# RMSNorm with swish on one core: row groups of unequal size, and three engines kept in the written order

## The chip, the cores and the metric

The kernel runs on one core of a Trainium2 chip. The time is device microseconds of one execution. Four engines matter here: ACT (ScalarE), DVE (VectorE), POOL (GpSimd), and SP (SyncE), which only issues DMA transfers in this kernel. TensorE does nothing.

## What is computed

`x` is 16 x 1024 x 512 float32, so 16384 rows of 512 values, `gamma` has 512 values and `eps` is a number.

```
rms = np.sqrt(np.mean(x ** 2, axis=-1, keepdims=True) + eps)
x_norm = x / rms * gamma
return (x_norm * (1.0 / (1.0 + np.exp(-x_norm)))).astype(np.float32)
```

## The kernel before

Each of the 128 partitions holds 128 whole rows, one after the other in memory. They are worked on in 16 tiles of `R = 8` rows a partition, so a tile is 128 x 4096 float32, 2.097 MB. A tile stays in one buffer `x_t` of a pool of eight from its load to its store; all steps work in place on it.

A tile goes through these steps, each written as a function with the tile's number:

- `issue_load` (L66): SP issues one transfer from HBM into `x_t`.
- `stage_sq` (L76): ACT squares each of the 8 rows and sums it into a column of `ms`, one instruction a row.
- `stage_rstd` (L89, L93): POOL adds eps to `ms` and raises it to the power -0.5, giving `rstd`, two small instructions of 128 x 8.
- `stage_z_sig` (L107, L116): DVE multiplies each row by its `rstd` and by `gamma`, one instruction a row; then ACT takes the sigmoid of the whole tile into `s_t` (two buffers).
- `stage_mul` (L128): DVE multiplies `x_t` by `s_t`, one instruction for the tile.
- `stage_store` (L139): SP issues one transfer back to HBM.

The loop at the end runs steps s = 0, 1, ...; in each it writes load s + 2, sq s, rstd s - 1, z and sigmoid s - 2, product s - 3, store s - 4. That is the order in which the work is written. The order in which each engine gets it is set by the framework's scheduler, which sorts ready work by its own estimate of times; on each engine the work is then done strictly in the order that came out, and waits are on semaphores. SP's queue is in order too: a transfer that waits holds back those behind it. In the order that came out, SP issues `gamma` and seven loads without a wait, and from there on a store and a load in turns; a load also waits until the store that last used its buffer has landed.

Each DMA transfer is spread over 16 DMA engines, and the transfers of one queue go through each of these one behind the other.

Of the kernel before, what the change touches and what calls it, by code (L numbers as in the profile page):

```python
# [1 line left out]

# [4 lines left out]

FP32 = mybir.dt.float32


@with_exitstack
def kernel(
    ctx: ExitStack,
    tc: tile.TileContext,
    x: bass.AP,
    gamma: bass.AP,
    eps: bass.AP,
    out: bass.AP,
):
    nc = tc.nc  # L20
    P = nc.NUM_PARTITIONS

    eps_val = float(eps)

    xf = x.flatten_outer_dims()
    of = out.flatten_outer_dims()
    N, D = xf.shape
    assert N % P == 0
    RPP = N // P
    x_v = xf.rearrange("(p n) d -> p n d", p=P)  # L30
    o_v = of.rearrange("(p n) d -> p n d", p=P)

    R = 8
    while RPP % R != 0:
        R //= 2
    R = max(R, 1)
    ntiles = RPP // R

    consts = ctx.enter_context(tc.tile_pool(name="consts", bufs=1))
    xpool = ctx.enter_context(tc.tile_pool(name="xpool", bufs=8))  # L40
    spool = ctx.enter_context(tc.tile_pool(name="spool", bufs=2))
    small = ctx.enter_context(tc.tile_pool(name="small", bufs=6))
    scratch = ctx.enter_context(tc.tile_pool(name="scratch", bufs=4))

    g_t = consts.tile([P, D], FP32)
    nc.sync.dma_start(out=g_t[:], in_=gamma.partition_broadcast(P))

    neghalf = consts.tile([P, R], FP32)
    nc.gpsimd.memset(neghalf[:], -0.5)  # L49
    eps_t = consts.tile([P, R], FP32)  # L50
    nc.gpsimd.memset(eps_t[:], eps_val)  # L51

    inv_sqrt_d = float(D) ** -0.5

    x_tiles: dict[int, bass.AP] = {}
    ms_tiles: dict[int, bass.AP] = {}
    rstd_tiles: dict[int, bass.AP] = {}
    s_tiles: dict[int, bass.AP] = {}

    PRE = 2  # L60

    def issue_load(i):
        if not (0 <= i < ntiles):
            return
        x_t = xpool.tile([P, R, D], FP32)
        nc.sync.dma_start(out=x_t, in_=x_v[:, i * R : (i + 1) * R, :])  # L66
        x_tiles[i] = x_t

    def stage_sq(i):
        if not (0 <= i < ntiles):  # L70
            return
        x_t = x_tiles[i]
        ms = small.tile([P, R], FP32)
        for r in range(R):
            sq_a = scratch.tile([P, D], FP32, tag="sqa")
            nc.scalar.activation(  # L76
                out=sq_a[:],
                in_=x_t[:, r, :],
                func=mybir.ActivationFunctionType.Square,
                scale=inv_sqrt_d,  # L80
                accum_out=ms[:, r : r + 1],
            )
        ms_tiles[i] = ms

    def stage_rstd(i):
        if not (0 <= i < ntiles):
            return
        ms = ms_tiles.pop(i)
        nc.gpsimd.tensor_tensor(  # L89
            out=ms[:], in0=ms[:], in1=eps_t[:], op=mybir.AluOpType.add  # L90
        )
        rstd = small.tile([P, R], FP32)
        nc.gpsimd.tensor_tensor(  # L93
            out=rstd[:],
            in0=ms[:],
            in1=neghalf[:],
            op=mybir.AluOpType.pow,
        )
        rstd_tiles[i] = rstd

    def stage_z_sig(i):
        if not (0 <= i < ntiles):
            return
        x_t = x_tiles[i]
        rstd = rstd_tiles.pop(i)
        for r in range(R):
            nc.vector.scalar_tensor_tensor(  # L107
                out=x_t[:, r, :],
                in0=x_t[:, r, :],
                scalar=rstd[:, r : r + 1],  # L110
                in1=g_t[:],
                op0=mybir.AluOpType.mult,
                op1=mybir.AluOpType.mult,
            )
        s_t = spool.tile([P, R, D], FP32)
        nc.scalar.activation(  # L116
            out=s_t[:],
            in_=x_t[:],
            func=mybir.ActivationFunctionType.Sigmoid,
        )  # L120
        s_tiles[i] = s_t

    def stage_mul(i):
        if not (0 <= i < ntiles):
            return
        x_t = x_tiles[i]
        s_t = s_tiles.pop(i)
        nc.vector.tensor_tensor(  # L128
            out=x_t[:],
            in0=x_t[:],  # L130
            in1=s_t[:],
            op=mybir.AluOpType.mult,
        )

    def stage_store(i):
        if not (0 <= i < ntiles):
            return
        x_t = x_tiles.pop(i)
        nc.sync.dma_start(out=o_v[:, i * R : (i + 1) * R, :], in_=x_t[:])  # L139

    for i in range(PRE):
        issue_load(i)

    nsteps = ntiles + 4
    for s in range(nsteps):
        issue_load(s + PRE)
        stage_sq(s)
        stage_rstd(s - 1)
        stage_z_sig(s - 2)
        stage_mul(s - 3)  # L150
        stage_store(s - 4)


# [1 line left out]
_INS = ['x', 'gamma', 'eps']  # L155
_OUTS = [((16, 1024, 512), 'float32')]
#: Inputs that are plain numbers.
_NUMBERS = {'eps': 9.999999747378752e-06}


# [26 lines left out]
```

## Time and profile before

| | |
|---|---|
| time, median of 4 runs | 201.62 us (201.45 to 201.84) |
| time of the profiled execution | 201.55 us |
| its span in the trace | 199.6 us |
| DVE busy | 155.1 us, 144 instructions |
| ACT busy | 138.5 us, 274 instructions |
| POOL busy | 58.9 us, 38 instructions |
| moved by DMA | 67.40 MB |

The span runs from the first to the last event of the core in the trace; the time of the execution is some 2 us longer. A time or a wait below is in microseconds from the span's start. The rows on which the prediction rests stand in a section of their own below.

### The profile page before, as it was taken

To read this page: it belongs to the slowest core of one execution; us is meant where nothing else is said; L and a number is where in the kernel's file an instruction comes from. 1 tells how busy PE (TensorE), PEld (TensorE's weight loads), DVE (VectorE), ACT (ScalarE), POOL (GpSimd) and SP (SyncE) were. 2 spreads that over 40 slices of the span, in tenths; PEclk is the share of its full clock that TensorE was granted. 3 is DMA by queue.
4 is the path that set the end of the run, shared out by engine and by line. 5 is a ranking of instruction groups with operands and counts; after the bars stand their busy time and mean duration, and the time that the engine had idled before them with its cause. 6 is when DMAs were issued, how large, how long until landed. Compare 5 with 4: busy or idle time off the path is not lost.

```text
span 199.6 us, 599 instructions
## 1 busy us (share of the span) xinstructions
DVE 155.1 (78%) x144; ACT 138.5 (69%) x274; POOL 58.9 (29%) x38
## 2 busy tenths in 40 slices
DVE  0004996999999999999969997899699967559350
ACT  2089799999999999529793976079956922940600
POOL 0003506408255283910584029100440030030000
DMA  5999999999999999999999999977910494054036
GB/s 151 424 430 424 437 437 425 417 433 404 368 305 433 435 420 427 424 427 437 414 432 427 430 427 433 433 322 332 446 72 0 210 420 210 0 210 210 0 151 269
DMA packets 4755, 67.40 MB, mean 338 GB/s; under 512 B 528, under 2 KB 528, under 8 KB 656
## 3 DMA queue, kind: packets, MB, share of 16 engines
q1 hardware_dynamic: 4752, 67.37, 81.0%
q14 instruction: 3, 0.02, 0.0%
HBM read 33.82 MB, written 33.55 MB: 337 GB/s over the span
## 4 chain that ended last, share of the span: by engine, by line
issue 40%; POOL 22%; DVE 5%; ACT 3%; POOLq 1%
POOL ms L89 12%; POOL rstd L93 9%; DVE x_t L107 3%; DVE x_t L128 2%; ACT s_t L116 2%; ACT sq_a L76 1%; POOLq L182 1%; POOLq L93 0%
## 5 line engine op out<-in xcount | busy, mean ns | idle before, releaser
L107 DVE SCALAR_TENSOR_TENSOR x_t<-x_t,rstd,g_t 128x512 f32<-128x512 f32 x128 | 86.2, 746 | 29.9 <-POOL rstd L93 29.9
L116 ACT ACTIVATE s_t<-x_t 128x4096 f32<-128x4096 f32 x16 | 57.8, 3611 | 40.1 <-DVE x_t L107 40.1
L76 ACT ACTIVATE sq_a<-x_t 128x512 f32<-128x512 f32 x128 | 78.4, 614 | 8.7 <-DMA x_t<-in_x_dram 8.7
L128 DVE TENSOR_TENSOR x_t<-x_t,s_t 128x4096 f32<-128x4096 f32 x16 | 70.5, 4419 | 7.4 <-ACT s_t L116 7.4
L89 POOL TENSOR_TENSOR ms<-ms,eps_t 128x8 f32<-128x8 f32 x16 | 28.9, 1806 | 118.2 <-ACT sq_a L76 118.2
L93 POOL TENSOR_TENSOR rstd<-ms,neghalf 128x8 f32<-128x8 f32 x16 | 29.6, 1853 | 1.3
L76 ACT ACTIVATION_READ_ACCUMULATOR sq_a<-x_t 128x1 f32 x128 | 23.9, 187 | 0.0
L76 ACT ACT_TABLE_LOAD x1 | 1.3, 1283 | 0.7 <-PEq L168 0.7
L116 ACT ACT_TABLE_LOAD x1 | 1.3, 1283 | 0.0
L49 POOL MEMSET neghalf<- 128x8 f32 x1 | 0.1, 106 | 0.3 <-POOLq L168 0.3
L168 POOL MEMSET const-float32-0.0<- 128x1 f32 x1 | 0.1, 99 | 0.2 <-issue 0.2
L51 POOL MEMSET eps_t<- 128x8 f32 x1 | 0.1, 105 | 0.0
L168 POOL MEMSET const-bfloat16-1.0<- 128x1 bf16 x1 | 0.1, 102 | 0.0
L168 POOL MEMSET const-uint8-127<- 128x1 uint8 x1 | 0.1, 102 | 0.0
L168 POOL MEMSET const-float32-1.0<- 128x1 f32 x1 | 0.1, 99 | 0.0
## 6 DMA issues: line engine op xcount, KB each, us to landing
x_t<-in_x_dram SPq DMA_DIRECT2D x16, 2048.0 KB, 15.3
out_dram<-x_t SPq DMA_DIRECT2D x16, 2048.0 KB, 11.5
g_t<-in_gamma_dram SPq DMA_DIRECT2D x1, 256.0 KB, 4.9
```

The lines of the kernel that those rows point to most:

```text
L49: nc.gpsimd.memset(neghalf[:], -0.5)
L51: nc.gpsimd.memset(eps_t[:], eps_val)
L76: nc.scalar.activation(out=sq_a[:], in_=x_t[:, r, :], func=mybir.ActivationFunctionType.Square, scale=inv_sqrt_d, accum_out=ms[:, r : r + 1],)
L89: nc.gpsimd.tensor_tensor(out=ms[:], in0=ms[:], in1=eps_t[:], op=mybir.AluOpType.add)
L93: nc.gpsimd.tensor_tensor(out=rstd[:], in0=ms[:], in1=neghalf[:], op=mybir.AluOpType.pow,)
L107: nc.vector.scalar_tensor_tensor(out=x_t[:, r, :], in0=x_t[:, r, :], scalar=rstd[:, r : r + 1], in1=g_t[:], op0=mybir.AluOpType.mult, op1= ...
L116: nc.scalar.activation(out=s_t[:], in_=x_t[:], func=mybir.ActivationFunctionType.Sigmoid,)
L128: nc.vector.tensor_tensor(out=x_t[:], in0=x_t[:], in1=s_t[:], op=mybir.AluOpType.mult,)
L168: nc = _bacc.Bacc("TRN2", target_bir_lowering=False, num_devices=1)
L182: with _tile.TileContext(nc) as tc:
```

## The change

Three things change.

The tiles get unequal sizes. `R` becomes the list `sizes`: 2, 2, 4, 4, 4 rows, then twelve tiles of 8, then 4, 4, 4, 2, 2, together 128 rows in 22 tiles. Each buffer keeps its full size (`RMAX` = 8 rows) and a small tile uses the first part of it. The pool of `x_t` grows from 8 to 9 buffers, that of `ms` and `rstd` from 6 to 8.

What stands ahead of the loop moves. The first two loads are written first; `gamma` is then loaded from ACT's queue, not SP's; the two constants of POOL's step are filled by DVE, not POOL; and a sigmoid of 128 x 8 values into an unused tile `warm` is put at the head of ACT's work.

The loop stands in a block that tells the scheduler to keep ACT, DVE and POOL in the order in which the work is written. SP's order is still made by the scheduler.

```diff
-    R = 8
-    while RPP % R != 0:
-        R //= 2
-    R = max(R, 1)
-    ntiles = RPP // R
+    RMAX = 8
+    if RPP >= 4 * 8 + 16:
...
+        sizes = [2, 2, 4, 4, 4] + [RMAX] * ((RPP - 32) // RMAX) + [4, 4, 4, 2, 2]
...
+    ntiles = len(sizes)
+    row0 = [0] * (ntiles + 1)
+    for i in range(ntiles):
+        row0[i + 1] = row0[i] + sizes[i]
...
-    xpool = ctx.enter_context(tc.tile_pool(name="xpool", bufs=8))
+    xpool = ctx.enter_context(tc.tile_pool(name="xpool", bufs=9))
...
-    small = ctx.enter_context(tc.tile_pool(name="small", bufs=6))
+    small = ctx.enter_context(tc.tile_pool(name="small", bufs=8))
...
-    g_t = consts.tile([P, D], FP32)
-    nc.sync.dma_start(out=g_t[:], in_=gamma.partition_broadcast(P))
-
-    neghalf = consts.tile([P, R], FP32)
-    nc.gpsimd.memset(neghalf[:], -0.5)
-    eps_t = consts.tile([P, R], FP32)
-    nc.gpsimd.memset(eps_t[:], eps_val)
...
-        x_t = xpool.tile([P, R, D], FP32)
-        nc.sync.dma_start(out=x_t, in_=x_v[:, i * R : (i + 1) * R, :])
+        R = sizes[i]
+        x_t = xpool.tile([P, RMAX, D], FP32)
+        nc.sync.dma_start(out=x_t[:, :R, :], in_=x_v[:, row0[i] : row0[i + 1], :])
...
     for i in range(PRE):
         issue_load(i)
 
+    g_t = consts.tile([P, D], FP32)
+    nc.scalar.dma_start(out=g_t[:], in_=gamma.partition_broadcast(P))
+    neghalf = consts.tile([P, RMAX], FP32)
+    nc.vector.memset(neghalf[:], -0.5)
+    eps_t = consts.tile([P, RMAX], FP32)
+    nc.vector.memset(eps_t[:], eps_val)
+    warm = consts.tile([P, RMAX], FP32)
+    nc.scalar.activation(
+        out=warm[:],
+        in_=neghalf[:],
+        func=mybir.ActivationFunctionType.Sigmoid,
+    )
+
     nsteps = ntiles + 4
-    for s in range(nsteps):
...
+    with tc.manual_schedule(engines={mybir.EngineType.Activation, mybir.EngineType.DVE, mybir.EngineType.Pool}):
+        for s in range(nsteps):
...
```

All other edits of the diff only cut a tile to its `R` rows (`x_t[:, :R, :]`).

The first place is the start of ACT's work. `sq_a` and `ms` are written by the squares, one instruction a row, `s_t` by the sigmoid. Before, on ACT:

```order
L76 ACT_TABLE_LOAD
L76 ACTIVATE sq_a,ms<-x_t 128x512 x16
L116 ACT_TABLE_LOAD
L116 ACTIVATE s_t<-x_t 128x4096
L76 ACTIVATE sq_a,ms<-x_t 128x512 x16
L116 ACTIVATE s_t<-x_t 128x4096
```

And in the changed kernel, on ACT:

```order
L161 DMA g_t<-in_gamma_dram 128x512
L167 ACT_TABLE_LOAD
L167 ACTIVATE warm<-neghalf 128x8
L83 ACTIVATE sq_a,ms<-x_t 128x512 x8
L128 ACTIVATE s_t<-x_t 128x1024
L83 ACTIVATE sq_a,ms<-x_t 128x512 x4
L128 ACTIVATE s_t<-x_t 128x1024
L83 ACTIVATE sq_a,ms<-x_t 128x512 x4
L128 ACTIVATE s_t<-x_t 128x2048
L83 ACTIVATE sq_a,ms<-x_t 128x512 x8
L128 ACTIVATE s_t<-x_t 128x2048
```

The first sigmoid comes after 8 rows of squares and not after 16, one table load is left, at the head, and from there squares and sigmoids come in turns.

The second place is the last part of DVE's work, where L107 (L119 in the changed kernel) is the scaled row and L128 (L141) the product with the sigmoid. Before, on DVE, the last rows:

```order
L107 SCALAR_TENSOR_TENSOR x_t<-x_t,rstd,g_t 128x512 x8
L128 TENSOR_TENSOR x_t<-x_t,s_t 128x4096 x2
L107 SCALAR_TENSOR_TENSOR x_t<-x_t,rstd,g_t 128x512 x16
L128 TENSOR_TENSOR x_t<-x_t,s_t 128x4096 x2
L107 SCALAR_TENSOR_TENSOR x_t<-x_t,rstd,g_t 128x512 x8
L128 TENSOR_TENSOR x_t<-x_t,s_t 128x4096
L107 SCALAR_TENSOR_TENSOR x_t<-x_t,rstd,g_t 128x512 x8
L128 TENSOR_TENSOR x_t<-x_t,s_t 128x4096
```

And in the changed kernel, on DVE, the last rows:

```order
L119 SCALAR_TENSOR_TENSOR x_t<-x_t,rstd,g_t 128x512 x8
L141 TENSOR_TENSOR x_t<-x_t,s_t 128x4096
L119 SCALAR_TENSOR_TENSOR x_t<-x_t,rstd,g_t 128x512 x4
L141 TENSOR_TENSOR x_t<-x_t,s_t 128x4096
L119 SCALAR_TENSOR_TENSOR x_t<-x_t,rstd,g_t 128x512 x4
L141 TENSOR_TENSOR x_t<-x_t,s_t 128x2048
L119 SCALAR_TENSOR_TENSOR x_t<-x_t,rstd,g_t 128x512 x4
L141 TENSOR_TENSOR x_t<-x_t,s_t 128x2048
L119 SCALAR_TENSOR_TENSOR x_t<-x_t,rstd,g_t 128x512 x2
L141 TENSOR_TENSOR x_t<-x_t,s_t 128x2048
L119 SCALAR_TENSOR_TENSOR x_t<-x_t,rstd,g_t 128x512 x2
L141 TENSOR_TENSOR x_t<-x_t,s_t 128x1024 x2
```

Each product now stands behind the scaled rows of the tile after its own, to the end, and before, the last products stood in pairs or right behind the scaled rows of their own tile.

## Rows read from the trace of the kernel before

**Rows 1.** The page: busy time by engine, and busy tenths in 40 slices.

```profile
DVE 155.1 (78%) x144; ACT 138.5 (69%) x274; POOL 58.9 (29%) x38
DVE  0004996999999999999969997899699967559350
DMA  5999999999999999999999999977910494054036
```

**Rows 2.** The waits: engine, line, what for: us in total, times, longest.

```profile
DVE x_t L107 <- POOL rstd L93: 29.9, 9, 17.8
```

**Rows 3.** Timeline of DVE: start, us, line, operation, count [idle before it].

```profile
73.47 5.38 DVE L107 SCALAR_TENSOR_TENSOR x_t<-x_t,rstd,g_t 128x512 f32<-128x512 f32 x8
78.77 4.42 DVE L128 TENSOR_TENSOR x_t<-x_t,s_t 128x4096 f32<-128x4096 f32 x1
83.11 5.39 DVE L107 SCALAR_TENSOR_TENSOR x_t<-x_t,rstd,g_t 128x512 f32<-128x512 f32 x8
...
98.05 4.42 DVE L128 TENSOR_TENSOR x_t<-x_t,s_t 128x4096 f32<-128x4096 f32 x1
104.28 5.39 DVE L107 SCALAR_TENSOR_TENSOR x_t<-x_t,rstd,g_t 128x512 f32<-128x512 f32 x8 [1.81 <-POOL rstd L93]
...
125.44 5.39 DVE L107 SCALAR_TENSOR_TENSOR x_t<-x_t,rstd,g_t 128x512 f32<-128x512 f32 x8 [1.81 <-POOL rstd L93]
130.75 8.76 DVE L128 TENSOR_TENSOR x_t<-x_t,s_t 128x4096 f32<-128x4096 f32 x2
141.42 5.39 DVE L107 SCALAR_TENSOR_TENSOR x_t<-x_t,rstd,g_t 128x512 f32<-128x512 f32 x8 [1.91 <-POOL rstd L93]
...
188.02 4.42 DVE L128 TENSOR_TENSOR x_t<-x_t,s_t 128x4096 f32<-128x4096 f32 x1 [3.68 <-ACT s_t L116]
```

**Rows 4.** Timeline of ACT over one tile.

```profile
40.05 0.61 ACT L76 ACTIVATE sq_a<-x_t 128x512 f32<-128x512 f32 x1
...
44.95 3.60 ACT L116 ACTIVATE s_t<-x_t 128x4096 f32<-128x4096 f32 x1
48.46 0.61 ACT L76 ACTIVATE sq_a<-x_t 128x512 f32<-128x512 f32 x1
```

**Rows 5.** Timeline of POOL.

```profile
15.84 0.20 POOL L89 TENSOR_TENSOR ms<-ms,eps_t 128x8 f32<-128x8 f32 x1 [14.96 <-ACT sq_a L76]
16.11 1.64 POOL L93 TENSOR_TENSOR rstd<-ms,neghalf 128x8 f32<-128x8 f32 x1
...
83.33 2.02 POOL L93 TENSOR_TENSOR rstd<-ms,neghalf 128x8 f32<-128x8 f32 x1
97.12 5.40 POOL L89 TENSOR_TENSOR ms<-ms,eps_t 128x8 f32<-128x8 f32 x1 [11.77 <-ACT sq_a L76]
...
123.77 1.64 POOL L93 TENSOR_TENSOR rstd<-ms,neghalf 128x8 f32<-128x8 f32 x1
```

**Rows 6.** Timeline of all engines, the first 20 us.

```profile
1.17 3.88 SPq L66 DMA_DIRECT2D x_t<-in_x_dram  x7
10.68 0.63 ACT L76 ACTIVATE sq_a<-x_t 128x512 f32<-128x512 f32 x1 [8.67 <-DMA x_t<-in_x_dram]
...
17.79 5.39 DVE L107 SCALAR_TENSOR_TENSOR x_t<-x_t,rstd,g_t 128x512 f32<-128x512 f32 x8 [17.79 <-POOL rstd L93]
```

**Rows 7.** Windows: stretch, us, DVE, ACT, POOL busy, PEclk, DMA share, GB/s.

```profile
0.00:2.50 2.50, 0.00 (x0) 1.28 (x1) 0.35 (x6) 1.00 0.18 49
2.50:5.00 2.50, 0.00 (x0) 0.00 (x0) 0.00 (x0) 1.00 0.97 252
5.00:7.50 2.50, 0.00 (x0) 0.00 (x0) 0.00 (x0) 1.00 1.01 426
40.00:60.00 20.00, 20.00 (x20) 20.00 (x46) 8.42 (x4) 1.00 0.99 378
60.00:120.00 60.00, 58.19 (x55) 48.51 (x94) 26.97 (x11) 1.00 1.01 428
```

**Rows 8.** Line 66, the loads: time from issue to landing.

```profile
DMA to landing us min/median/max: 9.5/15.3/35.6
```

More of the change, by code (lines that the diff above doesn't have):

```diff
@@ L71, in stage_sq @@
             return
+        R = sizes[i]
         x_t = x_tiles[i]
-        ms = small.tile([P, R], FP32)
+        ms = small.tile([P, RMAX], FP32)
         for r in range(R):
@@ L87, in stage_rstd @@
             return
+        R = sizes[i]
         ms = ms_tiles.pop(i)
         nc.gpsimd.tensor_tensor(
-            out=ms[:], in0=ms[:], in1=eps_t[:], op=mybir.AluOpType.add
+            out=ms[:, :R],
+            in0=ms[:, :R],
+            in1=eps_t[:, :R],
+            op=mybir.AluOpType.add,
         )
-        rstd = small.tile([P, R], FP32)
+        rstd = small.tile([P, RMAX], FP32)
         nc.gpsimd.tensor_tensor(
-            out=rstd[:],
-            in0=ms[:],
-            in1=neghalf[:],
+            out=rstd[:, :R],
+            in0=ms[:, :R],
+            in1=neghalf[:, :R],
             op=mybir.AluOpType.pow,
@@ L103, in stage_z_sig @@
             return
+        R = sizes[i]
         x_t = x_tiles[i]
@@ L114, in stage_z_sig @@
             )
-        s_t = spool.tile([P, R, D], FP32)
+        s_t = spool.tile([P, RMAX, D], FP32)
         nc.scalar.activation(
-            out=s_t[:],
-            in_=x_t[:],
+            out=s_t[:, :R, :],
+            in_=x_t[:, :R, :],
             func=mybir.ActivationFunctionType.Sigmoid,
@@ L125, in stage_mul @@
             return
+        R = sizes[i]
         x_t = x_tiles[i]
@@ L128, in stage_mul @@
         nc.vector.tensor_tensor(
-            out=x_t[:],
-            in0=x_t[:],
-            in1=s_t[:],
+            out=x_t[:, :R, :],
+            in0=x_t[:, :R, :],
+            in1=s_t[:, :R, :],
             op=mybir.AluOpType.mult,
@@ L137, in stage_store @@
             return
+        R = sizes[i]
         x_t = x_tiles.pop(i)
-        nc.sync.dma_start(out=o_v[:, i * R : (i + 1) * R, :], in_=x_t[:])
+        nc.sync.dma_start(
+            out=o_v[:, row0[i] : row0[i + 1], :], in_=x_t[:, :R, :]
+        )
     for i in range(PRE):
         issue_load(i)
-    nsteps = ntiles + 4
-    for s in range(nsteps):
[L146 to L151, printed above, removed]
+    g_t = consts.tile([P, D], FP32)
[9 more added lines that the diff above has]
+        func=mybir.ActivationFunctionType.Sigmoid,
+    )
+    nsteps = ntiles + 4
+    with tc.manual_schedule(engines={mybir.EngineType.Activation, mybir.EngineType.DVE, mybir.EngineType.Pool}):
+        for s in range(nsteps):
+            issue_load(s + PRE)
+            stage_sq(s)
+            stage_rstd(s - 1)
+            stage_z_sig(s - 2)
+            stage_mul(s - 3)
+            stage_store(s - 4)
 _INS = ['x', 'gamma', 'eps']
```

11 lines of the change are left out of this document (added).

## The prediction

> **What bounds the kernel now.** I read four views, from coarse to fine. The page comes first [rows 1]: DVE is busy 155.1 us of 199.6, and the slices show three stretches, an empty head of some 18 us, a middle in which DVE and the DMA engines are both full, and from about 120 us on a stretch in which DVE has holes and the DMA falls from full to a few tenths. So no engine is the bound over the whole span; the middle is bound, the two ends are lost time. The waits say who is late [rows 2]: DVE's rstd-scaled step (L107) waited 29.9 us for POOL, while POOL itself waits for ACT's sums of squares (11.77 us ahead of 97.12 [rows 5]).
>
> The DVE timeline gives the price of a tile [rows 3]: eight L107 instructions from 73.47 to 78.77 are 5.30 us (0.663 each), the product behind them runs from 78.77 to 83.11 in 4.34; together 9.64 us per 8 rows, 16 x 9.64 = 154 us in all. The DMA needs nearly the same: a tile is 2.097 MB in and as much out, at the 428 GB/s of 60 to 120 us [rows 7] 4.90 us each way, 9.80 a tile, 157 us in all. Both floors lie more than 40 us below the span. What is lost stands in the same rows: the first L107 starts at 17.79 [rows 6], and from 130.75 on DVE stops in front of nearly every tile (130.75 plus 8.76 is 139.51, the next one starts at 141.42, and so on), because the old order has ACT's squares stand behind a sigmoid that waits for DVE, so that neither runs ahead.
>
> In what follows a tile k has steps load, sq, rstd, z (the L107 lines), sig, mul, store. The new tiles 0 to 21 hold 2, 2, 4, 4, 4, then twelve times 8, then 4, 4, 4, 2, 2 rows.
>
> **The head.** The first load lands at 10.68 today, eight rows behind gamma [rows 6]. The landings behind it come 4.9 us apart: the first was 9.5 us on its way, the seventh 35.6 [rows 8], and seven issues take 3.88 [rows 6], so 26.1 + 3.3 lie between six landings. In the changed kernel tiles 0, 1 and 2 are those same eight rows, and gamma comes from ACT's queue beside them, not ahead. If gamma took nothing away, the bytes flow from about 1.9 us (49 GB/s over 2.5 us is 0.12 MB) and the eight rows are in at 6.8; if gamma still went first, at 10.7. By the volumes of rows 7, 0.12 + 0.63 + 1.07 = 1.82 MB are in by 7.5 us and 2.10 MB at 8.2. I take 8.3 for the landing of tile 2, with 6.8 and 10.7 as ends.
>
> From there ACT is the chain, since it now takes its work in the written order: sq 2, sig 0, sq 3, sig 1, sq 4, sig 2, sq 5, sig 3. That is 4 + 4 + 4 + 8 = 20 rows of sq at 0.613 (eight of them from 40.05 to 44.95 [rows 4]) = 12.3 us. For sig, 8 rows take 3.51 start to start [rows 4]; by proportion 2 rows take 0.88 and 4 rows 1.76, by a straight line through sq's 0.613 for one row and 3.51 for eight, 1.03 and 1.85. Two of each lie between 5.3 and 5.8; I take 5.5. So mul 3 can start at 8.3 + 12.3 + 5.5 = 26.1 us. The loads do not hold this chain: tiles 3, 4 and 5 land at 2.4, 4.9 and 9.8 us after tile 2, and their sq starts 3.4, 6.8 and 11.1 us after it. Until then DVE has done z 0 to 4 (16 rows) and mul 0 to 2 (8 rows), some 15 us of work, and has waited for the rest; what happens to DVE in there is hidden by ACT's chain, up to about 2 us. The second table load (1.28 us on ACT) and the memsets that leave POOL I cost at nothing: before the first landing ACT has nothing else to do.
>
> **The body.** From mul 3 on DVE has a backlog. It has left 112 rows of z, 112 x 0.663 = 74.2 us, and 120 rows of mul: by proportion 15 x 4.34 = 65.1, and with the fixed part that the line through one L107 row (0.663) and a product of eight gives (0.14 us) for the four instructions more than 15, 65.6. I take 65.2. For this to run without holes three things must hold. First, sig k must be there for mul k: it has z k+1 and mul k-1, 9.6 us, while ACT needs 8.4 a tile (40.05 to 48.46 [rows 4]). Second, rstd k must be there for z k: sq k now ends a sigmoid, a z and a mul earlier. In the rows in which POOL's add came 0.93 us ahead of a product, at 97.12 ahead of 98.05, it took 5.40 us, until the product had ended, and z started 1.81 us late [rows 3, 5]; here the same add would be parked just so, but the z behind it belongs to the tile before and has its rstd. Third, the loads: SP issues load j+7 behind store j, thus after mul j; with nine buffers it also waits for store j-2. ACT starts sq j+7 three z, two mul and one sig later: 15.9 + 8.7 + 3.5 = 28.1 us. Ahead of the load in the queue are at most four transfers of 4.90, with its own 24.5, and at most 2.3 us of issue and receipt (all that the last store takes beside its 4.9, below). That is 26.8, inside 28.1, and DVE's 9.64 against the DMA's 9.80 eats 0.16 x 12 = 1.9 us more. A late sq costs DVE nothing at first: mul j+5, the first to need it, starts 4.3 + 5.3 + 4.3 + 5.3 = 19.3 us after z j+4, and sig j+4, sq j+7 and sig j+5 are 11.9, so a load may come 7.4 us later still. The DMA as a whole ends at 1.9 + 157 = 159, before DVE.
>
> **The tail.** Today the last product ends at 192.44 [rows 3] and the span at 199.6, 7.2 us later, of which 4.9 is the transfer of eight rows. With two rows it is 7.2 - 4.9 + 1.2 = 3.5 us. mul 20 and mul 21 come back to back; sig 21 runs beside mul 20 (0.9 to 1.0 against 1.1), which costs 0.1 at most.
>
> **Sum.** 26.1 + 74.2 + 65.2 + 0.1 + 3.5 = 169.1 us of span. The profiled execution took 201.55 with a span of 199.6, so 1.95 us lie around the span; 201.55 is within 0.1 of the median of 201.62. The forecast is 169.1 + 1.95, about **171.1 us**.
>
> **A rule weighed against it.** POOL's power (L93) takes 1.64 us alone and 2.02 beside DVE's L107, and those eight L107 still take 5.39 us, at 83.11 with a power inside them and at 125.44 with none [rows 3, 5]. The Trainium skill, "SBUF — State Buffer", section "Who interferes with whom", says that a VectorE instruction with two SBUF inputs contends with a GpSimd one that reads SBUF, and that the later one blocks wholly ("Issue order, not op shape, decides who blocks"). For the add behind a product the trace agrees (5.40 us); for L107 behind a power it does not. By the rule the sum would be the last rival below, by the rows nothing is added.
>
> **Rivals.**
> (1) The DMA becomes the bound: its pace slips until the loads come later than the 28.1 + 7.4 us. For it: the window from 40 to 60 us moved 378 GB/s with the DMA engines 0.99 busy [rows 7], so there the transfers themselves were slower, and 20 us cost 2.3. Against it: the next 60 us have 428. At 400 GB/s over the whole run the transfers take 168.5 us from 1.9 on, and 2.3 us of receipt and program end make 172.7, 174.7 with the time around; at 390, 179. I price it at 176.
> (2) A power that has started when a product becomes ready holds it back. No row shows the pair (every power before ran beside L107 or alone). A product would lose from 0 to 2.02 us. The add would start 3.51 + 4.90 and some 0.2 of hand-over (an estimate), 8.6 us, after a z, the product 9.64 after it; if the add gets through in 0.3, the power lasts 1.3 us into the product. The product then starts later, and at the next tile the power fits in front of it, so every second tile pays: 7 x 1.3 = 9 us, 180 us. Against it: about 1 us ahead is where the add was parked at 97.12, and no power followed until the product had ended.
> (3) The small tiles give nothing and only the order works: first z at 17.8 as today, 154.3 of DVE, 3.5 of tail and 0.5 of waits give 176.1, 178 us. It needs a first landing near 10.7 for two rows.
> (4) Slower than before: POOL and DVE exclude each other at every meeting, L107 included. The 22 pairs of add and power (0.20 + 1.64 at least) would stand in DVE's line: 22 x 1.84 = 40 us, 211 us. It decides from 30.5 / 22 = 1.4 us a tile on. The 5.39 of rows 3 with and without a power speaks against it.
>
> **How the numbers follow.** The forecast has 0.70, with its own range from 169.2 to 173.7: down by a landing of tile 2 at 6.8, up by one at 10.7. An outcome still lower, below 169.2, gets 0.06. Rival 1 has 0.10, rival 2 0.07, rival 3 0.04, rival 4 0.03. The range from 169.2 to 178.0 takes in the forecast and most of rivals 1 and 3, 0.81. A measurement of this kernel can tell about 0.2% from no change. Faster has 0.96, same 0.01, slower 0.03.
>
> **What would show it.** Right: the first z at about 8 us; mul 3 (the second product of 128x2048) at about 26; from there DVE without holes until about 165, 9.6 us a tile; the DMA full until about 140 and then in bursts; waits of DVE for POOL under 5 us in total, all in the first 20 us; POOL's add long, beside products, with nobody waiting. Wrong: holes of DVE before z or mul in the body (rivals 2, 4, or an rstd that is late), ACT waiting for x_t after 30 us (rival 1), or a first z after 12 us (rival 3).

## The result and the profile after

The changed kernel takes 176.47 us (median of 9 runs, 175.51 to 176.59), against 201.48 before: a ratio of 0.874, 95% interval 0.873 to 0.876. That is 25.0 us less; forecast were 30.4 less, 171.1 us, with a range to 178.0. The profiled execution took 176.55 us with a span of 174.7, so the span is 5.6 us longer than the sum of 169.1.

The page of the changed kernel, busy time and slices, to be laid beside [rows 1]:

```profile
DVE 155.5 (89%) x152; ACT 138.3 (79%) x280; POOL 106.1 (61%) x48
DVE  0067798999969999999999999999999999999971
ACT  3479999999999999899797979797947658735420
DMA  5999999999999999999999999999999694788556
```

DVE does the same work, 155.5 us, and has lost its holes at the end. POOL is busy for 106.1 us where it was 58.9, with hardly more to do. The waits of the changed kernel (engine, line, what for: us in total, times, longest), beside [rows 2]; L119 is the scaled row z, L141 the product, L83 the square:

```profile
ACT s_t L128 <- DVE x_t L119: 24.9, 13, 3.9
DVE x_t L119 <- POOL rstd L104: 12.1, 5, 8.2
ACT sq_a L83 <- DMA x_t<-in_x_dram: 5.2, 2, 4.0
DVE x_t L141 <- ACT s_t L128: 2.5, 2, 1.7
```

ACT waits for data twice, both times in the head, and never in the body. DVE waits five times for POOL. Where, its timeline shows (start, us, line, operation, count [idle before]), beside [rows 3]:

```profile
9.11 1.42 DVE L119 SCALAR_TENSOR_TENSOR x_t<-x_t,rstd,g_t 128x512 f32<-128x512 f32 x2 [8.20 <-POOL rstd L104]
...
28.53 2.29 DVE L141 TENSOR_TENSOR x_t<-x_t,s_t 128x2048 f32<-128x2048 f32 x1 [0.85 <-ACT s_t L128]
...
38.24 5.38 DVE L119 SCALAR_TENSOR_TENSOR x_t<-x_t,rstd,g_t 128x512 f32<-128x512 f32 x8
43.64 4.42 DVE L141 TENSOR_TENSOR x_t<-x_t,s_t 128x4096 f32<-128x4096 f32 x1
49.59 5.39 DVE L119 SCALAR_TENSOR_TENSOR x_t<-x_t,rstd,g_t 128x512 f32<-128x512 f32 x8 [1.53 <-POOL rstd L104]
...
97.78 5.38 DVE L119 SCALAR_TENSOR_TENSOR x_t<-x_t,rstd,g_t 128x512 f32<-128x512 f32 x8
103.08 4.42 DVE L141 TENSOR_TENSOR x_t<-x_t,s_t 128x4096 f32<-128x4096 f32 x1
107.42 5.38 DVE L119 SCALAR_TENSOR_TENSOR x_t<-x_t,rstd,g_t 128x512 f32<-128x512 f32 x8
...
167.14 1.41 DVE L119 SCALAR_TENSOR_TENSOR x_t<-x_t,rstd,g_t 128x512 f32<-128x512 f32 x2 [0.87 <-POOL rstd L104]
168.47 2.49 DVE L141 TENSOR_TENSOR x_t<-x_t,s_t 128x1024 f32<-128x1024 f32 x2
```

The row at 28.53 is mul 3, forecast for 26.1. From there DVE runs without a hole but for 1.53 us ahead of z 7 (49.59) and 0.87 ahead of z 21 (167.14), at 9.64 us a tile (97.78 to 107.42). POOL's timeline at these two places (add L97, power L104), beside [rows 5]:

```profile
40.18 3.50 POOL L97 TENSOR_TENSOR ms<-ms,eps_t 128x8 f32<-128x8 f32 x1 [3.89 <-ACT sq_a L83]
43.76 5.80 POOL L104 TENSOR_TENSOR rstd<-ms,neghalf 128x8 f32<-128x8 f32 x1
...
158.93 7.40 POOL L97 TENSOR_TENSOR ms<-ms,eps_t 128x2 f32<-128x2 f32 x1 [3.35 <-ACT sq_a L83]
166.40 0.70 POOL L104 TENSOR_TENSOR rstd<-ms,neghalf 128x2 f32<-128x2 f32 x1
```

The add of tile 7, an operation of 0.20 us, starts at 40.18 beside z 6 (38.24) and ends only when z 6 does; the power is then held for all of the product at 43.64. The add of tile 21 stands through z 19, mul 18, z 20 and mul 19.

The windows of the head (stretch, us, DVE, ACT, POOL busy, PEclk, DMA share, GB/s), beside [rows 7]:

```profile
2.50:5.00 2.50, 0.00 (x0) 0.17 (x1) 0.00 (x0) 1.00 0.92 261
5.00:7.50 2.50, 0.00 (x0) 0.82 (x3) 0.00 (x0) 1.00 0.98 343
7.50:10.00 2.50, 0.89 (x2) 1.85 (x6) 1.32 (x4) 1.00 1.01 426
```

Full pace comes 2.5 us later than in the kernel before, which had 426 GB/s from 5.0 us on.

### The profile page after: what moved, and what is told of

Read it like the earlier page. It is cut to its first block, busy times and chain, and to the rows that moved or that the text cites. A ratio compares the mean times of both kernels' runs of the same rounds, so it can differ in the third digit from the quotient of the medians.

```text
span 174.7 us, 652 instructions
## 1 busy us (share of the span) xinstructions
DVE 155.5 (89%) x152; ACT 138.3 (79%) x280; POOL 106.1 (61%) x48
## 4 chain that ended last, share of the span: by engine, by line
POOL 51%; issue 22%; ACT 2%; DVE 2%; POOLq 1%; ACTq 0%
POOL ms L97 33%; POOL rstd L104 17%; ACT sq_a L83 1%; DVE x_t L119 1%; DVE x_t L141 1%; ACT s_t L128 1%; POOLq L212 0%; POOLq L104 0%; ACTq L128 0%
## 5 line engine op out<-in xcount | busy, mean ns | idle before, releaser
L119 DVE SCALAR_TENSOR_TENSOR x_t<-x_t,rstd,g_t 128x512 f32<-128x512 f32 x128 | 86.6, 741 | 12.1 <-POOL rstd L104 12.1
L97 POOL TENSOR_TENSOR ms<-ms,eps_t 128x8 f32<-128x8 f32 (+2 forms) x22 | 61.0, 2772 | 59.0 <-ACT sq_a L83 59.0
L83 ACT ACTIVATE sq_a<-x_t 128x512 f32<-128x512 f32 x128 | 78.4, 613 | 5.3 <-DMA x_t<-in_x_dram 5.2
L128 ACT ACTIVATE s_t<-x_t 128x4096 f32<-128x4096 f32 (+2 forms) x22 | 58.9, 2679 | 24.9 <-DVE x_t L119 24.9
L141 DVE TENSOR_TENSOR x_t<-x_t,s_t 128x4096 f32<-128x4096 f32 (+2 forms) x22 | 71.5, 3251 | 2.6 <-ACT s_t L128 2.5
L104 POOL TENSOR_TENSOR rstd<-ms,neghalf 128x8 f32<-128x8 f32 (+2 forms) x22 | 45.0, 2046 | 1.7
L83 ACT ACTIVATION_READ_ACCUMULATOR sq_a<-x_t 128x1 f32 x128 | 23.9, 186 | 0.0
```

What stands on the lines that cost most here:

```text
L83: nc.scalar.activation(out=sq_a[:], in_=x_t[:, r, :], func=mybir.ActivationFunctionType.Square, scale=inv_sqrt_d, accum_out=ms[:, r : r + 1],)
L97: nc.gpsimd.tensor_tensor(out=ms[:, :R], in0=ms[:, :R], in1=eps_t[:, :R], op=mybir.AluOpType.add,)
L104: nc.gpsimd.tensor_tensor(out=rstd[:, :R], in0=ms[:, :R], in1=neghalf[:, :R], op=mybir.AluOpType.pow,)
L119: nc.vector.scalar_tensor_tensor(out=x_t[:, r, :], in0=x_t[:, r, :], scalar=rstd[:, r : r + 1], in1=g_t[:], op0=mybir.AluOpType.mult, op1= ...
L128: nc.scalar.activation(out=s_t[:, :R, :], in_=x_t[:, :R, :], func=mybir.ActivationFunctionType.Sigmoid,)
L141: nc.vector.tensor_tensor(out=x_t[:, :R, :], in0=x_t[:, :R, :], in1=s_t[:, :R, :], op=mybir.AluOpType.mult,)
```

## The experiments

Each kernel is the changed one with the edit shown, unless said otherwise.

**What the order and the sizes are each worth.** `order_only` has sixteen tiles of 8 rows in the written order.

```diff
-        sizes = [2, 2, 4, 4, 4] + [RMAX] * ((RPP - 32) // RMAX) + [4, 4, 4, 2, 2]
+        sizes = [RMAX] * (RPP // RMAX)
```

> The changed kernel with sixteen tiles of 8 rows, so the written order of ACT, DVE and POOL is the only large thing left of the change. Theory (order and sizes each pay for their own place, the order for the body, the sizes for head and tail): the first z at about 16.5, since the first load still brings 8 rows; then ACT's chain sq 1, sq 2, sig 0 puts mul 0 at about 28, z 0 and z 1 lie before it, 14 x 5.30 + 16 x 4.34 = 143.6 us are left, 7.2 of tail: a span of 179, 181 us. DVE without holes from 28 us on. Rival (the small tiles are what lets the loads run smoothly, or POOL is late at every tile without them): holes of 1 to 2 us per tile, 190 us or more.

Measured: 182.5 us, two runs at about 181.5 and two at about 183.5, ratio 0.906, interval 0.901 to 0.911. The profiled execution is one of the first two. Its DVE waits:

```profile
16.75 5.39 DVE L119 SCALAR_TENSOR_TENSOR x_t<-x_t,rstd,g_t 128x512 f32<-128x512 f32 x8 [15.86 <-POOL rstd L104]
22.35 5.39 DVE L119 SCALAR_TENSOR_TENSOR x_t<-x_t,rstd,g_t 128x512 f32<-128x512 f32 x8 [0.21 <-POOL rstd L104]
28.10 4.42 DVE L141 TENSOR_TENSOR x_t<-x_t,s_t 128x4096 f32<-128x4096 f32 x1 [0.36 <-ACT s_t L128]
```

These are all it has: after 28.10 the order alone keeps DVE full to the end. The theory holds: its span is 179.5 us where 179 was forecast. What makes two of the four runs 1.9 us longer, no trace shows. What stands ahead of the loop is changed here too, but mul 0, which started at 28.70 us in the kernel before, starts only 0.6 us earlier, so nearly all of the gain is the order.

`head_sizes` has the small tiles at the head alone.

```diff
+        sizes = [2, 2, 4, 4, 4] + [RMAX] * ((RPP - 16) // RMAX)
```

> The changed kernel with small tiles at the head alone: 2, 2, 4, 4, 4, then fourteen of 8 rows. Theory (the small last tiles spare 3.5 us of the last transfer and cost DVE 0.9 us of waiting for POOL at the last tile, which goes with them): 176.5 + 3.5 - 0.9 = 179.1 us. Rival (the small last tiles give nothing, as the DMA had work queued at the end anyway): 175.6 to 176.5 us.

Measured: 179.70 us (179.68 to 179.80), ratio 0.891, interval 0.890 to 0.893, and no wait of DVE after 49.63 us. So the small last tiles are worth 3.2 us, and the wait that they bring ahead of z 21 is inside that.

`tiles_only` has the sizes, but the scheduler's order.

```diff
-    with tc.manual_schedule(engines={...}):
+    if True:
```

(The set of the three engines is left out of the line above.)

> The changed kernel without the block that keeps the written order: the scheduler orders ACT, DVE and POOL. Theory (the order pays for the body's end): holes of DVE as before from about 110 us on, since squares of 16 rows again stand between two sigmoids; the head gains some 9 us (first z at 9, not 17.8) and the tail 3.5, so 201.5 - 12.5 = 189 us. Rival (the sizes do it all): within 1% of 176.5.

Measured: 205.99 us, ratio 1.022, interval 1.021 to 1.024: slower than the kernel before, and the theory falls with its 189. Its waits:

```profile
POOL ms L97 <- ACT sq_a L83: 132.0, 21, 18.8
ACT s_t L128 <- DVE x_t L119: 53.1, 17, 7.5
DVE x_t L119 <- POOL rstd L104: 31.2, 16, 9.4
DVE x_t L141 <- ACT s_t L128: 10.9, 6, 3.7
```

The head does gain (the first z starts at 10.33 us, after a wait of 9.43, and not at 17.79), but DVE then waits 21.8 us for POOL in 15 places and 10.9 for sigmoids, where the kernel before waited 12.1 us in 8 places and 7.4. In the scheduler's order z often stands right behind its own rstd, so that a wait is as long as a power, with or without the add before it (1.8 to 1.9 us in seven of the places), and more tiles are more such places.

`tiles_psum` was to tell how much of that is POOL: `tiles_only`, with gamma copied to PSUM as in `gamma_psum` below.

> The scheduler's order with the unequal tiles, and gamma read from PSUM by z, so that z no longer holds POOL back. Theory (the time of 206 us with the scheduler's order comes from squares, power, z, sigmoid and product of one tile standing one behind the other, POOL's delays being 0 to 3 us of it): 203 to 206 us. Rival (POOL held back by z is what makes it slow): 195 us or less.

Measured: 190.61 us (190.58 to 190.70), ratio 0.946. The theory falls, but the run doesn't prove the rival either: with another operand the scheduler also came to another order on ACT and DVE, so order and POOL changed together. How the 206 divides between them stays open.

**The head: gamma.** `no_gamma` has no transfer of gamma; DVE fills the tile with ones, so the input gamma is left out.

```diff
-    nc.scalar.dma_start(out=g_t[:], in_=gamma.partition_broadcast(P))
+    nc.vector.memset(g_t[:], 1.0)
```

> The changed kernel without the transfer of gamma: DVE fills its tile with ones, so that gamma's input is left out. Theory (gamma's 128 packets beside the first loads hold them back, that is the 2.3 us by which tile 2 landed later than forecast): tile 0 lands at about 4.5 and not 6.7, tile 2 at about 8.2 and not 10.6, and mul 3 starts 2.3 us earlier: 174.2 us. Rival (the first microseconds of any transfer are slow, gamma or not): tile 2 still lands after 10 us and the time is 176 to 176.5.

Measured: 174.03 us (173.21 to 175.33), ratio 0.866; the profiled execution is the fastest of the four, and what spreads them over 2.1 us is not known. ACT's first squares of tiles 0 and 2 in the changed kernel, and then in `no_gamma`:

```profile
6.68 0.63 ACT L83 ACTIVATE sq_a<-x_t 128x512 f32<-128x512 f32 x1 [4.01 <-DMA x_t<-in_x_dram]
10.64 0.63 ACT L83 ACTIVATE sq_a<-x_t 128x512 f32<-128x512 f32 x1 [1.22 <-DMA x_t<-in_x_dram]
```

```profile
4.25 0.63 ACT L83 ACTIVATE sq_a<-x_t 128x512 f32<-128x512 f32 x1 [2.02 <-DMA x_t<-in_x_dram]
8.04 0.63 ACT L83 ACTIVATE sq_a<-x_t 128x512 f32<-128x512 f32 x1 [1.22 <-DMA x_t<-in_x_dram]
```

Tile 2 is there 2.60 us earlier, and mul 3 starts at 25.92 and not 28.53. The theory holds. This trace, like that of `gamma_rows`, also lacks the wait of 0.87 us ahead of z 21, so gamma's cost is read from the starts in the head and not from the times.

`gamma_rows` asks why: the same 128 packets of 2 KB, each from another row of x (so the scaling by gamma is not computed).

```diff
-    nc.scalar.dma_start(out=g_t[:], in_=gamma.partition_broadcast(P))
+    nc.scalar.dma_start(out=g_t[:], in_=x_v[:, 0, :])
```

> The changed kernel with the transfer of gamma reading 128 different rows of x in place of the one row of gamma 128 times (so the scaling by gamma is wrong; packets, bytes and queue stay the same). Theory (what holds the first loads back is that all packets read the same 2 KB): the transfer then costs its bytes, 0.26 MB at 428 GB/s = 0.6 us, tile 2 lands at 8.0 + 0.6 = 8.6 and the time is 174.6 to 175 us. Rival (128 packets of 2 KB beside the first loads cost this whatever they read): tile 2 lands at 10.6 as now, 176.5 us.

Measured: 173.83 us (173.64 to 173.96), and tile 2 at

```profile
8.66 0.63 ACT L83 ACTIVATE sq_a<-x_t 128x512 f32<-128x512 f32 x1 [1.24 <-DMA x_t<-in_x_dram]
```

That is 8.04 plus the 0.6 us of its bytes. So it is not the small packets: reading one and the same 2 KB 128 times costs 2.0 us more than reading 128 different rows. Why the same row is slower, no run here tells.

`gamma_first` puts gamma back at the head of SP's queue.

> The changed kernel with gamma again issued first on SP's queue, as before the change. Theory (beside the loads or ahead of them, gamma's packets hold the slowest of the 16 DMA engines back by the same): tile 2 lands at 10.5 to 10.9 and the time stays within 0.5 us of 176.5. Rival (moving gamma to ACT's queue did help): tile 2 later by 1 us or more, 177.5 us or more.

Measured: 176.20 us (175.83 to 176.33). The first square of tile 2:

```profile
11.43 0.63 ACT L83 ACTIVATE sq_a<-x_t 128x512 f32<-128x512 f32 x1 [1.24 <-DMA x_t<-in_x_dram]
```

That is 0.8 us later than in the changed kernel, between the two theories. The time doesn't show it, since this trace has no wait ahead of z 21.

**POOL held back by z.** `gamma_psum` lets ACT copy gamma into PSUM once, so that z has one full operand in SBUF and not two (its column of `rstd` stays there).

```diff
+    g_sb = g_t
+    psum = ctx.enter_context(tc.tile_pool(name="psum", bufs=1, space=bass.MemoryType.PSUM))
+    g_ps = psum.tile([P, D], FP32)
+    nc.scalar.copy(out=g_ps[:], in_=g_sb[:])
+    g_t = g_ps
```

> The changed kernel with gamma copied once to PSUM by ACT, so that z reads one operand from SBUF and one from PSUM. Theory (POOL's add and power are held back for as long as DVE runs an instruction with two SBUF operands, z included; this made z 7 late by 1.5 us and z 21 by 0.9): adds beside z take about 0.2 us, none is parked before the product starts, and the two waits go: 174 to 175 us, if z costs the same 0.663 us from PSUM. If it costs more, 128 times the difference is added. Rival (only the product holds POOL back): the adds beside z stay long and nothing is gained, 176.5 or more.

Measured: 173.88 us (173.78 to 173.91), ratio 0.863, interval 0.861 to 0.864. POOL's and DVE's timelines at tile 7:

```profile
40.14 0.20 POOL L97 TENSOR_TENSOR ms<-ms,eps_t 128x8 f32<-128x8 f32 x1 [4.78 <-ACT sq_a L83]
40.42 1.64 POOL L104 TENSOR_TENSOR rstd<-ms,neghalf 128x8 f32<-128x8 f32 x1
```

```profile
38.17 5.35 DVE L119 SCALAR_TENSOR_TENSOR x_t<-x_t,rstd,g_ps 128x512 f32<-128x512 f32 x8
43.60 4.43 DVE L141 TENSOR_TENSOR x_t<-x_t,s_t 128x4096 f32<-128x4096 f32 x1
47.94 5.35 DVE L119 SCALAR_TENSOR_TENSOR x_t<-x_t,rstd,g_ps 128x512 f32<-128x512 f32 x8
```

At the same moment, 40.14, beside the same z 6, the add takes 0.20 us and not 3.50, and z 7 starts without a wait. POOL's busy time over the span falls from 106.1 to 43.3 us, DVE waits for POOL once, for the first z, and z costs the same. Beside a product, whose two operands are still in SBUF, the add is held as before, until the product has ended:

```profile
82.01 4.42 DVE L141 TENSOR_TENSOR x_t<-x_t,s_t 128x4096 f32<-128x4096 f32 x1
82.17 4.32 POOL L97 TENSOR_TENSOR ms<-ms,eps_t 128x8 f32<-128x8 f32 x1 [3.57 <-DVE x_t L119]
```

The theory holds. The Trainium skill, "SBUF — State Buffer", section "Who interferes with whom", says that a DVE instruction with at most one SBUF input, outside DVE's 2-port modes, does not contend with GpSimd. The rows at tile 7 agree: 0.20 us for the add beside z.

**The ninth buffer.** `bufs8` takes it away.

```diff
-    xpool = ctx.enter_context(tc.tile_pool(name="xpool", bufs=9))
+    xpool = ctx.enter_context(tc.tile_pool(name="xpool", bufs=8))
```

> The changed kernel with eight buffers of x_t as before, not nine. Theory (the loads have some 7 us to spare): SP waits longer for stores to land (4.0 us in all with nine), ACT and DVE do not notice, 176.5 us. Rival (the ninth buffer is what keeps the loads ahead): ACT waits for x_t in the body, DVE has holes, 178 us or more.

Measured: 175.70 us (175.60 to 175.78). SP waits 78.5 us for stores to land, not 4.0, and ACT still waits for x_t only in the head. The theory holds: the ninth buffer gives nothing. The 0.8 us less go with the wait of 0.87 ahead of z 21, which this trace doesn't have. The add of tile 21 starts at the same time as in the changed kernel, but is held for 3.86 us and not for 7.40:

```profile
158.94 3.86 POOL L97 TENSOR_TENSOR ms<-ms,eps_t 128x2 f32<-128x2 f32 x1 [3.35 <-ACT sq_a L83]
```

The traces of `no_gamma`, `gamma_rows` and `gamma_first` have 3.86 there too. The nine runs of the changed kernel lie in two groups, six at 176.4 to 176.6 and three at 175.5 to 175.6; that they differ by this wait fits, but no trace of the second group was taken.

**Both losses removed.** `pe_gamma` loads gamma once, 2 KB into one partition, and spreads it to 128 partitions in PSUM by one TensorE product.

```diff
-    g_t = consts.tile([P, D], FP32)
-    nc.scalar.dma_start(out=g_t[:], in_=gamma.partition_broadcast(P))
+    psum = ctx.enter_context(tc.tile_pool(name="psum", bufs=1, space=bass.MemoryType.PSUM))
+    g_row = consts.tile([1, D], FP32)
+    ones = consts.tile([1, P], FP32)
+    nc.vector.memset(ones[:], 1.0)
+    g_t = psum.tile([P, D], FP32)
+    nc.scalar.dma_start(out=g_row[:], in_=gamma.partition_broadcast(1))
+    nc.tensor.matmul(g_t[:], lhsT=ones[:], rhs=g_row[:], start=True, stop=True)
```

> The changed kernel with gamma loaded once into one partition (2 KB) and spread to 128 partitions in PSUM by one TensorE product with a row of ones; z reads it there. Theory (the two losses are separate: 2.3 to 2.6 us of gamma's packets in the head, 2.4 to 2.6 us of POOL held back by z): both go, 176.5 - 2.5 - 2.5 = 171.5 us, runs within 0.2 us of each other. Rival (the gains overlap, since what DVE waits for in the head hides the one behind the other): 173 to 174 us, as each of them alone.

Measured: 171.68 us (171.12 to 172.21), ratio 0.851, interval 0.848 to 0.854. The median is what the theory says: the gains add up. The runs spread over 1.1 us, which it did not: in the profiled one tile 2 is squared from 9.14 us and not 8.0, and what held that load back is not known.

`pe_sizes` is `pe_gamma` with finer tiles at both ends.

```diff
+        sizes = [2, 2, 2, 2, 4, 4, 4, 4] + [RMAX] * ((RPP - 40) // RMAX) + [4, 4, 2, 2, 2, 1, 1]
```

> The kernel with gamma spread by TensorE, and finer tiles at both ends: 2, 2, 2, 2, 4, 4, 4, 4, then eleven of 8, then 4, 4, 2, 2, 2, 1, 1 rows. Theory (after the first z DVE loses what ACT's squares of the next two tiles keep a sigmoid back: 5.0 us in two waits; and the end waits for a transfer of two rows): the two waits fall to some 2.5 us together, the last transfer by 0.6, five more products cost 0.5: 171.2 - 2.6 = 168.6 us. Rival (seven tiles ahead are now 20 rows and not 32, and the loads fall behind): ACT waits for x_t after 15 us, and the time is 171 or more.

Measured: 169.18 us (168.94 to 169.63), ratio 0.840, interval 0.838 to 0.842, the fastest of all. DVE's waits for sigmoids fell from 5.0 to 1.9 us, and ACT has no wait for x_t after the first tile.

## Why the prediction was right, and where it was off

The time lies in the range, and its mechanism, an end set by DVE's work behind a short head, is what the trace shows. That the number lies in the range is partly luck. The forecast was 5.4 us low, and 176.5 lies above the forecast's own range of 169.2 to 173.7, in the part that was added for rivals 1 and 3, and neither of these happened. Two losses that the sum did not have, one in the head and one at POOL, took their place. Step by step, in the order of the sum:

- **Landing of tile 2**, forecast 8.3 us, measured 10.6 (the start of its squares, for which ACT waited): 2.3 us, the first of the two errors. The step that failed counts the volumes of [rows 7] up to the 2.10 MB of the eight rows. Gamma's 0.26 MB are in those volumes too and were not added, and the moment at which a volume is reached was taken for the landing. On the kernel before, the same count puts gamma and its first eight rows, 2.36 MB, at 8.8 us, and ACT started on them at 10.68 [rows 6], so there the count is 1.9 us early. The runs show what gamma costs: tile 2 comes at 8.04 without it (`no_gamma`), 0.6 us later for its bytes and another 2.0 for reading one row 128 times (`gamma_rows`). The upper end of 10.7 was met, but not for its reason: it stood for gamma going first, and with gamma first tile 2 came at 11.43.
- **ACT's chain** of 20 rows of squares and four sigmoids, forecast 17.8 us: from 10.64 to 28.49, 17.85. Right. From start to start, as in the forecast, the two sigmoid sizes took 0.94 to 0.95 and 1.80, in the middle of the bounds: 5.49 for the four, where 5.5 was taken.
- **DVE's work from mul 3 on**, forecast 139.4 us: 28.53 to 170.96, 142.4. Of the 3.0 us, 1.53 and 0.87 are the waits for POOL, and 0.1 is z 6 to its product; the rest is instructions that cost 0.5 us more than the sum. The step that failed is the second of the three conditions: "sq k now ends a sigmoid, a z and a mul earlier". In the body that is so, and there the adds are held for 5.40 us with nobody waiting, as forecast. It fails at two places. At tile 7 ACT has no lead yet: sq 7 ends during z 6, and only mul 5 lies between that and z 7. At tile 21 the tiles are so small that a z and a mul are over soon. At tile 7 add and power stand from 40.18 to 49.56, 9.4 us for what takes 1.9 when nothing holds it (`gamma_psum`), and at tile 21 from 158.93 to 167.10, 8.2 us for some 1.0. These delays of 7.5 and 7.2 us are more than the lead, some 6 us at both. At tile 21 it was close: in four other traces the add got through after 3.86 us and nobody waited.
- **What holds POOL.** From [rows 3, 5] I took it that only the product does. The add was held beside z as well, and `gamma_psum` shows that it is z's second SBUF operand. The trace of the kernel before had it already: the z ahead of the product at 98.05 (the row below) runs to 98.12, and the add that starts at 97.12 [rows 5], and takes 0.20 us alone, stood beside it for 0.9 us before the product began. What the text said of the other direction, that DVE's z does not pay for a power beside it, stayed right: 5.38 to 5.39 us with a power inside and without.

```profile
92.74 5.38 DVE L107 SCALAR_TENSOR_TENSOR x_t<-x_t,rstd,g_t 128x512 f32<-128x512 f32 x8
```

- **The loads**: right that they are in time. ACT never waited for x_t in the body, and with eight buffers neither. How much of the 7 us to spare was left is not measured.
- **The tail**, forecast 3.5 us: 170.96 to 174.7, 3.7. **Around the span**, 1.95: 1.85.

The rivals: the DMA was not the bound (1); the product was never held back by a power, it was the other way round: the products at 43.64 and 148.62 took 4.42 and 4.41 us, and the powers beside them 5.80 and 5.73 (2); the small tiles at the head are worth 2.8 us (`order_only` 182.5 against `head_sizes` 179.7; 2.0 between the spans of the two profiled executions) and at the tail 3.2 (3); POOL did not exclude DVE (4). Of the signs that were named, "waits of DVE for POOL under 5 us, all in the first 20" was wrong: 12.1 us in all, of which 8.20 is the first z, and 2.4 come late. These 2.4 us are also the sign of being wrong that was named, holes of DVE before z from an rstd that is late, in two places.

The 25 us come so: 19.0 by the order (201.5 to `order_only`'s 182.5, and 18 to 20 by its single runs; gamma's move and the warm table are in this too, and its first z came 1.0 us earlier, at 16.75), the other 6 by the sizes. The sizes without the order cost 4.5. So the two parts don't simply add: the written order is what makes small tiles pay.

## What to carry to other kernels

Where two engines are both nearly full and the end of the trace shows holes, look first at the order in which each engine gets its work, which was worth 19 of the 25 us here; keep each step of a tile at least one whole tile of work behind the step that feeds it, and check that lead separately where the pipeline fills and where tiles get small. When a small operation on GpSimd sits between ScalarE and VectorE, look at its longest and not at its mean duration, and give VectorE an operand from PSUM if it holds GpSimd back. A constant that is broadcast from HBM by many packets of one row is better loaded into one partition and spread on the chip, as in `pe_gamma`; to put it behind the first loads was not tried.

## What the runs showed of the hardware that was not expected

- A power of POOL alone takes 0.70 us for 128 x 2, 1.01 for 128 x 4 and 1.64 for 128 x 8; the add takes 0.20 for each. Beside DVE instructions with two SBUF operands the same add took between 0.21 us (at 147.89) and 7.86. Sometimes it gets through between two instructions of z, sometimes it is held to the end of the product behind them; which of the two, no run here tells.

```profile
138.25 7.86 POOL L97 TENSOR_TENSOR ms<-ms,eps_t 128x4 f32<-128x4 f32 x1 [7.30 <-ACT sq_a L83]
...
147.89 0.21 POOL L97 TENSOR_TENSOR ms<-ms,eps_t 128x4 f32<-128x4 f32 x1 [0.31 <-ACT sq_a L83]
```

- 128 reads of one 2 KB row cost 2.0 us more than 128 reads of different rows, and the loads beside them, which are in another queue, pay for it (tile 0 is squared from 6.68 against 4.72 us, tile 2 from 10.64 against 8.66).
- z with one operand from PSUM costs what it costs from SBUF: eight in 5.35 us against 5.38.
